# Streaming modulation weights in row pieces behind the input, on one Trainium2 core

## The chip, the cores and the metric

The kernel runs on one core of one Trainium2 chip. The metric is the device time of one execution in microseconds (us); 944.57 us is the median of three runs of the kernel before (942.94 to 949.04).

## The reference

One layer of a hybrid block on x (1024 tokens by 1024 channels), all in float32. Only the first lines matter for this change:

```
mod = c @ w_ada[l] + b_ada[l]                       # 1024 -> 3 x 1024
shift, scale, gate = jnp.split(mod, 3, axis=-1)
h = _rmsnorm(x, norm_g[l]) * (1.0 + scale[:, None, :]) + shift[:, None, :]
proj = h @ w_in[l]                                  # 1024 x 6152 columns
...
x = x + gate[:, None, :] * (merged @ w_out[l])
```

Behind the projection come two attentions with eight heads each (stick-breaking and forgetting), gates, an output projection and a last norm.

## The kernel before

The kernel keeps h transposed in SBUF, channels on partitions, as eight blocks of 128 channels by 1024 tokens. Each block is held as a rounded part and a remainder (`hhi`, `hlo`), and so is each weight (`split`: a copy on ScalarE that rounds, a subtraction that leaves the rest). A product of 128 channels is three matmuls of 128x512 (`mm3`).

The change is in the start, the code under `tc.tile_pool(name="start")`. It is written as small steps, and the string `SEQ` (L44) gives the order in which they are issued; each engine works through its own queue in an order that the scheduler makes from it. A letter is a step, a digit its block:

- `X` loads 128 tokens of x (512 KB). `s` sums their squares on ScalarE. `n` makes the reciprocal root for four of these blocks (`n0` for tokens 0 to 511, `n1` for 512 to 1023): a Ln and an Exp on ScalarE and small steps on VectorE.
- `x` scales a block and turns it on TensorE, 128x128 at a time, eight squares in two PSUM banks; a copy on ScalarE or VectorE (string `CPY`, L41) takes each bank to `xnT`. Blocks in `DIAG` (L38) are not scaled first but multiplied by a diagonal matrix that holds the factors (L268).
- `L` loads modulation weights, `a` multiplies them by c and adds over the eight row blocks on VectorE (`weigh`, L279 and L281), `f` (`factors`) adds over the 128 partitions with a matmul against ones (L292) and makes shift and scale of one channel block on VectorE (L294, L295).
- `m` modulates a block on ScalarE (L301) and splits it. `R` and `w` load and split the first four column blocks of `w_in`; `POOLW` (L39) names those whose subtraction runs on GpSimd.
- `p` multiplies one channel block by the four weights into seven PSUM banks: 21 matmuls of 128x512 for each of the eight blocks, 168 in all.

Before, `L` brings all 1024 rows of 128 columns of shift and of scale (one `L` brings 256), in two DMAs of 512-byte rows, and the loads are mixed with those of x: the first comes ahead of all but one x block. `a`, `f`, `m` and `p` of a channel block follow as its weights are there.

All loads go through SyncE's queue. Its DMAs carry one of eight semaphores, so that a DMA waits for the one eight places ahead of it. The raw weights of `w_in` share three buffers.

Behind the start come 24 matmuls for one more bank (L1011), the values' projection (L530 to L532) and the attentions. There the order of the instructions on every engine is not touched by the change.

Of the kernel before, what the change touches and what calls it, by code (L numbers as in the profile page):

```python
# [8 lines left out]
F32 = mybir.dt.float32  # L9
# [5 lines left out]
ALU = mybir.AluOpType  # L15
# [24 lines left out]
BATCH = (4,)  # L40
CPY = "dd aa aa aa ad dd ad aa"  # L41
GROUPS = ((0,), (1,), (2,), (3, 4), (5,), (6,), (7,))
ADATAG = ("ada1", "ada1b", "ada1", "ada2", "xb1", "ada1b", "ada1")
SEQ = "X2 L0 X0 s0 X1 X3 X4 s3 a0 X7 s2 X6 X5 s1 n0 x0 L1 s4 s5 s7 s6 R0 L2 x2 f0 R2 L3 n1 x1 a3 a1 x3 x4 R1 w0 x5 f1 x7 x6 R3 m0l w1l L6 w1r m0r m1l m1r a2 w3l L5 w2 f2 a5 f3 m2 m3l a6 p0l p1l f4 p0r w3r p1r m3r f5 p2l L7 f6 m4 m5l p2r p3l p3r a7 f7 m6 m5r m7l p4 p5 p6l p6r m7r p7"  # L44
WPOOL = ()
MLAG = 2
GAHEAD = 1
# [21 lines left out]
def tile_hybrid_block(ctx, tc, x, c, w_ada, b_ada, norm_g, w_in, b_forget,  # L69
                      w_o_sb, w_o_fox, b_gate, w_out, final_g, out):  # L70
    nc = tc.nc
    x2 = x[0]
    out2 = out[0]
    wada = w_ada[0]
# [58 lines left out]
    cT = cols[:, 0:8]  # L133
# [25 lines left out]
    def load_raw(src, shape, name="wraw"):  # L159
        raw = wpool.tile(shape, F32, name=name, tag="wraw", bufs=3)  # L160
        nc.sync.dma_start(raw, src)
        return raw

    def split(hi, lo, raw, pool=False):
        nc.scalar.copy(hi, raw)  # L165
        (nc.gpsimd if pool else nc.vector).tensor_sub(lo, raw, hi)  # L166
        return hi, lo

    def load_w(src, shape, pool=False):
# [27 lines left out]
    with tc.tile_pool(name="start", bufs=1) as sp:  # L197
# [2 lines left out]
        xt = [xa[:, t, :] for t in range(4)] + [xb[t // 2][:, t % 2, :] for t in range(4)]  # L200
        xnT = sp.tile([P, KB, S], F32, name="xnT")
        half = {"": slice(0, S), "l": slice(0, 512), "r": slice(512, S)}
        group = {k: g for g in GROUPS for k in g}
        edges = (0,) + BATCH + (TB,)
        batch = {t: b for b in range(len(edges) - 1) for t in range(edges[b], edges[b + 1])}
        adas, ams, raws, norms, sums, wsplit, bank = {}, {}, {}, {}, {}, {}, [0]
# [2 lines left out]
        def load_x(t):  # L209
            nc.sync.dma_start(xt[t], x2[t * P:(t + 1) * P, :])  # L210

        def load_ada(k):
            n = len(group[k]) * P
            tag = ADATAG[GROUPS.index(group[k])]
            ada = sp.tile([P, KB, 2, n], F32, name="ada", tag=tag, bufs=1)
            for j in range(2):
                nc.sync.dma_start(ada[:, :, j, :],
                                  wada[:, j * D + k * P: j * D + k * P + n].rearrange("(q p) n -> p q n", p=P))
            adas[k] = ada

        def load_w0(i):
            raws[i] = load_raw(wcol((QA, KA, GCOL + 8 * P, ZA)[i]), WSH)
# [33 lines left out]
        def turn_x(t):  # L256
            if t in DIAG:
                diag = sp.tile([P, P], F32, name="diag", tag="diag", bufs=2)
                nc.vector.tensor_scalar(diag, ident, norms[t], None, ALU.mult)
            else:  # L260
                (nc.gpsimd if t in POOLX else nc.vector).tensor_scalar(xt[t], xt[t], norms[t], None, ALU.mult)
            for b in range(2):
                copy = nc.scalar.copy if CPY.split()[t][b] == "a" else nc.vector.tensor_copy
                pt = turn_tile(t)
                for k in range(4):
                    o, i = pt[:, k * P:(k + 1) * P], xt[t][:, (4 * b + k) * P:(4 * b + k + 1) * P]
                    if t in DIAG:
# [5 lines left out]
        def weigh(k):

            n = len(group[k]) * P
            if k in PEK:
                return
            o = ams[k] = sp.tile([P, 2, n], F32, name="am", tag="am%d" % n, bufs=2)
            nc.vector.tensor_scalar(o, adas[k][:, 0], cT[:, 0:1], None, ALU.mult)  # L279
            for q in range(1, KB):  # L280
                nc.vector.scalar_tensor_tensor(o, adas[k][:, q], cT[:, q:q + 1], o, ALU.mult, ALU.add)  # L281

        def factors(k):
            k0 = group[k][0]
            pm = acc_tile(2)
            for j in range(2):
                if k in PEK:
                    for q in range(KB):
                        nc.tensor.matmul(pm[:, j:j + 1], adas[k][:, q, j, :], cT[:, q:q + 1], start=q == 0,
                                         stop=q == KB - 1)  # L290
                    continue
                nc.tensor.matmul(pm[:, j:j + 1], ams[k0][:, j, (k - k0) * P:(k - k0 + 1) * P], ones,  # L292
                                 start=True, stop=True)
# [10 lines left out]
        def split_w(i, part):  # L304
# [158 lines left out]
    def largest(p):  # L463


        pt = tp_tile()
        nc.tensor.transpose(pt[0:1, :P], vmost[p], ident)
        top = at.tile([1, 1], F32, name="vtop", tag="vtop", bufs=2)
        nc.vector.tensor_reduce(top, pt[0:1, :P], mybir.AxisListType.X, ALU.max)
        nc.vector.tensor_scalar(top, top, 1e-25, None, ALU.max)  # L470
        e = top.bitcast(I32)
        nc.vector.tensor_scalar(e, e, 0x7F800000, None, ALU.bitwise_and)
        pair = vscale[p] = at.tile([1, 2], F32, name="vpow", tag="vpow", bufs=2)
        nc.vector.tensor_scalar(pair[:, 0:1].bitcast(I32), e, -1.0, float((254 + VSCALE) << 23), ALU.mult, ALU.add)
        nc.vector.tensor_scalar(pair[:, 1:2].bitcast(I32), e, 1.0, float((VSCALE + 15) << 23), ALU.mult, ALU.subtract)

    def spread(p):

        pt = tp_tile()
        nc.tensor.matmul(pt[:, 0:2], ones_row, vscale[p], start=True, stop=True)  # L480
        o = at.tile([P, 2], F32, name="vsc", tag="vsc", bufs=2)
        nc.vector.tensor_copy(o, pt[:, 0:2])
        for q in (p, p + 1):
            vscale[q], vback[q] = o[:, 0:1], o[:, 1:2]

    def sprinkle(units, marks):
# [12 lines left out]
        return units  # L499
# [51 lines left out]
    def load_v(p):  # L551
        vraw[p] = load_raw(vd[p], [P, S], "vraw").rearrange("p (a b d) -> p a b d", a=TB, b=2)
# [471 lines left out]
    for p in range(7):  # L1024
        a, b = [], []
        if p == 0:
            g = sprinkle(gs.pop(0), [(6, lambda: load_v(0)), (8, lambda: largest(0)), (10, lambda: spread(0)),
                                     (13, lambda: take_v(0))])
# [12 lines left out]
        q = p + 1  # L1041
# [39 lines left out]
    for t in range(TB):  # L1081
# [12 lines left out]
        for i, (c0, c1) in enumerate(zip(cuts, cuts[1:])):  # L1094
            n = slice(c0, c1)
# [53 lines left out]
```

## Time and profile before

| | |
|---|---|
| median of three runs | 944.57 us |
| the profiled execution's own time | 944.57 us |
| its span (first to last instruction) | 942.9 us |
| first of the 168 matmuls of the start | 30.96 us |
| first matmul behind them (L1011) | 79.04 us |

Times in rows are microseconds from the start of the span unless a row says ns. PE is TensorE, PEld its weight load, DVE VectorE, ACT ScalarE, POOL GpSimd, SP SyncE. The end of a matmul is modelled: a matmul of 128x512 is shown with some 0.4 us, while the next one starts 0.23 us later. So spacing is read from starts. A float32 matmul (not the rounded kind) shows as two instructions.

### The profile page before, as it was taken

Reading aid. Unit: us, or ns where it says so; the run is one execution under the profiler, and the core shown is the slowest. Engines: PE = TensorE matmul, PEld = TensorE weight load, DVE = VectorE, ACT = ScalarE, POOL = GpSimd, SP = SyncE. Lnnn points to the kernel's source line nnn. Section 1 sums busy time; section 2 is a strip of 40 time slices with the busy share of each in tenths; the row PEclk is TensorE's granted clock in tenths of the full one; section 3 lists DMA queues with packets and bytes.
Section 4 is the critical chain, followed back from the end, with each engine's and each line's share of the span. In section 5 each row is a group of like instructions: output and inputs, shape, how many; then the busy total and the mean of one; then the engine's idle time right before and its main releaser. Section 6 shows DMA issues by size and latency. Waiting matters only on the chain. (4 is left out here: it accounts for less than half of the span.)

```text
span 942.9 us, 14905 instructions
## 1 busy us (share of the span) xinstructions
PE 891.2 (95%) x5282; PEld 753.0 (80%) x5282; DVE 704.8 (75%) x1402; ACT 598.3 (63%) x1102; POOL 115.8 (12%) x191
## 2 busy tenths in 40 slices
PE   2799999999999989999999999999999999999997
PEld 2688978889788868889878787897887777788886
DVE  4984998688786788878798768657687767776544
ACT  5656787776777697897678765445667456553222
POOL 0401001000010000100000112211212212540000
PEclk9999999999999989999999999999999999999999
DMA  9933495544594564936548697967999999552221
GB/s 313 305 98 101 100 225 122 127 104 121 132 193 121 143 152 112 176 82 133 147 121 187 175 211 157 210 160 188 192 203 173 279 263 213 201 178 90 101 92 54
DMA packets 260659, 152.14 MB, mean 161 GB/s; under 512 B 157156, under 2 KB 241748, under 8 KB 260584
## 3 DMA queue, kind: packets, MB, share of 16 engines
q1 hardware_dynamic: 257592, 142.78, 60.5%
q0 software_dynamic: 2880, 8.39, 4.9%
q8 instruction: 41, 0.67, 0.3%
q14 instruction: 34, 0.28, 0.1%
q10 hardware_dynamic: 112, 0.02, 0.0%
HBM read 80.31 MB, written 24.71 MB: 111 GB/s over the span
## 5 line engine op out<-in xcount | busy, mean ns | idle before, releaser
L181 PE MATMUL acc<-hhi,w 128*128 128x512 f32 x584 | 237.4, 406 | 0.0
L183 PE MATMUL acc<-hhi,w 128*128 128x512 f32 x584 | 230.0, 394 | 0.0
L182 PE MATMUL acc<-hlo,w 128*128 128x512 f32 x584 | 229.7, 393 | 0.0
L183 PEld LDWEIGHTS acc<-hhi,w 128*128 128x128 f32 x584 | 110.8, 190 | 24.6
L726 DVE SCALAR_TENSOR_TENSOR pc<-pw,pc 128x1024 f16<-128x1024 f32 (+7 forms) x128 | 96.6, 758 | 43.2 <-ACT pc L722 42.4
L181 PEld LDWEIGHTS acc<-hhi,w 128*128 128x128 f32 x584 | 111.4, 191 | 21.7 <-issue 2.0
L182 PEld LDWEIGHTS acc<-hlo,w 128*128 128x128 f32 x584 | 111.3, 191 | 19.6
L722 ACT ACTIVATE pc<-pw 128x1024 f16<-128x1024 f32 (+7 forms) x128 | 86.8, 679 | 19.2 <-DMA wT<-pc 17.8
L718 ACT ACTIVATE pw<-pw,low 128x1024 f32<-128x1024 f32 (+3 forms) x64 | 49.6, 776 | 73.3 <-DVE low L713 73.3
L766 POOL TENSOR_TENSOR ysb<-ysb,fac 128x128 f32<-128x128 f32 x64 | 35.6, 556 | 452.1 <-DVE ysb L765 388.1
L720 ACT ACTIVATE pw<-pw,low 128x1024 f32<-128x1024 f32 (+3 forms) x64 | 49.5, 774 | 62.1 <-DVE low L713 61.7
L530 PE MATMUL acc<-wv,hhi 128*128 128x256 f32 (+1 forms) x256 | 73.6, 288 | 0.0
L532 PE MATMUL acc<-wv,hlo 128*128 128x256 f32 (+1 forms) x256 | 72.4, 283 | 0.0
L531 PE MATMUL acc<-wv,hhi 128*128 128x256 f32 (+1 forms) x256 | 72.4, 283 | 0.0
L701 DVE SCALAR_TENSOR_TENSOR pw<-z,pw 128x512 f32<-128x512 f32 (+4 forms) x96 | 52.9, 553 | 23.1 <-ACT pw L692 22.6
L756 PE MATMUL pv<-vv,wT 128*128 128x128 f16 x534 | 66.6, 220 | 3.7 <-DVE ysb L765 3.7
L623 PE MATMUL z<-ks,qs 128*128 128x512 f32 (+1 forms) x192 | 66.4, 346 | 2.7 <-DVE yT L778 2.7
L625 PE MATMUL z<-kx,qs 128*128 128x512 f32 (+1 forms) x192 | 65.7, 344 | 3.4 <-DMA kx<-ks 3.4
L757 PE MATMUL pv<-vv,wT 128*128 128x128 f16 x534 | 66.5, 220 | 0.0
L166 DVE TENSOR_TENSOR w<-wraw,w 128x1024 fp32r<-128x1024 f32 x44 | 54.0, 1227 | 10.0 <-ACT w L165 8.8
L757 PEld LDWEIGHTS <-wT 128*128 128x128 f16 x576 | 56.6, 98 | 4.4 <-issue 4.1
L708 DVE TENSOR_TENSOR_SCAN pw<-pw 128x512 f32<-128x512 f32 (+2 forms) x64 | 58.9, 921 | 1.2
(276 smaller groups left out, 1985.8 us busy)
## 6 DMA issues: line engine op xcount, KB each, us to landing
wraw<-in_w_in_dram SPq DMA_DIRECT2D x48, 512.0 KB, 4.7
gd<-stg SPq DMA_DIRECT2D x32, 256.0 KB, 2.6
kx<-ks POOLq DMA_DIRECT2D x28, 256.0 KB, 6.4
ada<-in_w_ada_dram SPq DMA_DIRECT2D x12, 512.0 KB, 7.6
zd<-stg SPq DMA_DIRECT2D x16, 256.0 KB, 2.8
zt<-zd SPq DMA_DIRECT2D x32, 128.0 KB, 2.7
vraw<-vd SPq DMA_DIRECT2D x8, 512.0 KB, 3.9
fb<-fd SPq DMA_DIRECT2D x8, 512.0 KB, 4.6
```

Source lines behind the costliest of these rows:

```text
L181: nc.tensor.matmul(ps, w[0], x[0], start=first, stop=False)
L182: nc.tensor.matmul(ps, w[0], x[1], start=False, stop=False)
L183: nc.tensor.matmul(ps, w[1], x[0], start=False, stop=last)
L530: nc.tensor.matmul(ps[:, a], hhi[k][:, t], hi[:, k, :], start=k == 0, stop=False)
L531: nc.tensor.matmul(ps[:, a], hhi[k][:, t], lo[:, k, :], start=False, stop=False)
L532: nc.tensor.matmul(ps[:, a], hlo[k][:, t], hi[:, k, :], start=False, stop=k == KB - 1)
L623: nc.tensor.matmul(o, qs[p, j][:, tq], ks[p, j][:, s], start=True, stop=False)
L625: nc.tensor.matmul(o, qs[p, j][:, tq], kx[p, j][:, s], start=False, stop=not mask)
L722: nc.scalar.activation(pair.parts(a)[0], w, AF.Copy, scale=WSCALE)
L726: nc.vector.scalar_tensor_tensor(lo, pair.logits(a), WSCALE, hi, ALU.mult, ALU.subtract)
L756: nc.tensor.matmul(y[:, a, :], w[:, b + s, :], v, start=s == 0, stop=False)
L757: nc.tensor.matmul(y[:, a, :], w[:, b + nb + s, :], v, start=False, stop=s == nb - 1)
```

## The change

`L` now brings pieces of 256 rows by 512 columns of shift and of scale, in two DMAs of 2048-byte rows: eight pieces, the first four for channel blocks 0 to 3, the last four for blocks 4 to 7, in three buffers. All x blocks are loaded ahead of them. `a` makes two VectorE steps of 128x1024 for a piece. The factors of blocks 0 to 3 are made together when their four pieces are weighed, and so are those of blocks 4 to 7. x blocks 5 and 7 are also turned with a diagonal; all bank copies but the two of block 0 run on ScalarE; all subtractions of the weights run on VectorE. A new step `d` (`warm`) issues four float32 matmuls of 128x512 into a bank that nothing reads; `d0` and `d1` stand behind the turns and ahead of the factors. The preload of the values' weights is put behind the last split.

```diff
-DIAG = (1, 4, 6)
-POOLW = (0, 1, 2, 3)
+DIAG = (1, 4, 5, 6, 7)
+POOLW = ()
-CPY = "dd aa aa aa ad dd ad aa"
-GROUPS = ((0,), (1,), (2,), (3, 4), (5,), (6,), (7,))
-SEQ = "X2 L0 X0 s0 X1 X3 X4 s3 a0 X7 s2 X6 X5 s1 n0 x0 L1 s4 ...
+CPY = "dd aa aa aa aa aa aa aa"
+SEQ = "X2 X0 s0 X1 X3 X4 s3 X7 s2 X6 X5 s1 L0 L1 n0 x0 L2 s4 s5 s7 s6 a0 x2 L3 R0 n1 x1 a1 x3 x4 R1 a2 L4 w0 x5 x7 x6 d0 d1 a3 R2 L5 f0 m0l w1l f1 ...
-        def load_ada(k):
...
+        def load_ada(i):
+
+            ada = adas[i] = sp.tile([P, 2, 2, 512], F32, name="ada", tag="ada", bufs=3)
+            rows_ = wada[i % 4 * 2 * P:(i % 4 + 1) * 2 * P, :]
             for j in range(2):
+                c0 = j * D + i // 4 * 512
+                nc.sync.dma_start(ada[:, :, j, :], rows_[:, c0:c0 + 512].rearrange("(q p) n -> p q n", p=P))
...
+        def weigh(i):
+
+            g = i // 4
+            if i % 4 == 0:
+                ams[g] = sp.tile([P, 2, 512], F32, name="am", tag="am", bufs=2)
+            for x in range(2):
+                q = i % 4 * 2 + x
+                if q == 0:
+                    nc.vector.tensor_scalar(ams[g], adas[i][:, x], cT[:, 0:1], None, ALU.mult)
+                else:
+                    nc.vector.scalar_tensor_tensor(ams[g], adas[i][:, x], cT[:, q:q + 1], ams[g], ALU.mult, ALU.add)
...
+        def warm(k):
+
+            o = acc_tile(2)
+            for i in range(4):
+                nc.tensor.matmul(o, ident, xnT[:, k, 512:1024], start=i == 0, stop=i == 3)
...
-    first_v[0].preload()
+    with tc.issue_after(last_split[0].ins), tc.issue_after(last_split[1].ins):
+        first_v[0].preload()
```

`warm` and `factors` both take the one PSUM bank of `acc_tile(2)`.

On TensorE, at the end of the turns (L270 and L268 before, L266 after), the kernel before has:

```order
L270 MATMUL z<-ident,xb_169 128x128 x4
L270 MATMUL tp<-ident,xb_170 128x128 x4
L181 MATMUL z<-hhi,wqk 128x512
L270 MATMUL acc<-ident,xb_170 128x128 x4
L181 MATMUL acc<-hhi,wz 128x512
L268 MATMUL z<-diag,xb_170 128x128 x4
L268 MATMUL tp<-diag,xb_170 128x128 x4
```

and the changed one:

```order
L266 MATMUL z<-diag,xb_170 128x128 x4
L266 MATMUL tp<-diag,xb_170 128x128 x4
L324 MATMUL acc<-xnT,ident 128x512 x8
L286 MATMUL acc<-ones,am 128x1 x8
L180 MATMUL z<-hhi,wqk 128x512 x2
L180 MATMUL acc<-hhi,wz 128x512
```

The first projections (L181, now L180) stood between the last turns; now they stand behind the eight unread matmuls (L324) and behind the factors' matmuls of four channel blocks (L286).

On VectorE, around the factors of the blocks that TensorE needs first, the kernel before has (`am_399` and `am_284` are weighed sums, `hlo_157` and `hlo_158` the remainders of blocks 0 and 1):

```order
L166 TENSOR_TENSOR hlo_157<-xnT_171,hhi_149 128x512
L166 TENSOR_TENSOR hlo_158<-xnT_171,hhi_150 128x512
L279 TENSOR_SCALAR am_284<-ada_259,cols_128 128x512
L281 SCALAR_TENSOR_TENSOR am_399<-ada_236,cols_128,am_399 128x256
L281 SCALAR_TENSOR_TENSOR am_284<-ada_259,cols_128,am_284 128x512
...
L294 TENSOR_TENSOR ashf_142<-acc_417,cols_128 128x1
L295 SCALAR_TENSOR_TENSOR amul_141<-acc_417,b_scale1_132,cols_128 128x1
```

and the changed one (`am_228` is the sum of pieces 0 to 3, `am_401` that of pieces 4 to 7, `wz_407` the third weight):

```order
L281 SCALAR_TENSOR_TENSOR am_228<-ada_244,cols_128,am_228 128x1024 x2
L165 TENSOR_TENSOR wqk_312<-wraw_247,wqk_312 128x1024
L165 TENSOR_TENSOR wqk_312<-wraw_305,wqk_312 128x256
L165 TENSOR_TENSOR wqk_312<-wraw_305,wqk_312 128x768
L279 TENSOR_SCALAR am_401<-ada_309,cols_128 128x1024
L281 SCALAR_TENSOR_TENSOR am_401<-ada_309,cols_128,am_401 128x1024
L288 TENSOR_TENSOR ashf_142<-acc_368,cols_128 128x1
L289 SCALAR_TENSOR_TENSOR amul_141<-acc_368,b_scale1_132,cols_128 128x1
L288 TENSOR_TENSOR ashf_142<-acc_378,cols_128 128x1
L289 SCALAR_TENSOR_TENSOR amul_141<-acc_378,b_scale1_132,cols_128 128x1
L165 TENSOR_TENSOR wz_407<-wraw_363,wz_407 128x1024
L288 TENSOR_TENSOR ashf_142<-acc_394,cols_128 128x1
```

The subtractions of the weights (L165) came from GpSimd, and the third one now stands between the factors of block 1 and those of block 2.

On SyncE's queue, the kernel before begins with:

```order
L210 DMA xa_168<-in_x_dram 128x1024
L217 DMA ada_173<-in_w_ada_dram 128x8x128 x2
L210 DMA xa_168<-in_x_dram 128x1024 x3
L210 DMA xb0_169<-in_x_dram 128x1024
L210 DMA xb1_170<-in_x_dram 128x1024 x2
```

and the changed one with (`wraw` are the first weights of `w_in`):

```order
L209 DMA xa_168<-in_x_dram 128x1024 x4
L209 DMA xb0_169<-in_x_dram 128x1024
L209 DMA xb1_170<-in_x_dram 128x1024 x2
L209 DMA xb0_169<-in_x_dram 128x1024
L217 DMA ada_189<-in_w_ada_dram 128x2x512 x2
L217 DMA ada_192<-in_w_ada_dram 128x2x512 x2
L217 DMA ada_216<-in_w_ada_dram 128x2x512 x2
L217 DMA ada_244<-in_w_ada_dram 128x2x512 x2
L159 DMA wraw_247<-in_w_in_dram 128x8x128
```

Two transfers of modulation weights that stood behind the first x block now stand behind the last one.

## Rows read from the trace of the kernel before

**Rows 1.** The page: busy time by engine, then slices of the span (40)
```profile
PE 891.2 (95%) x5282; PEld 753.0 (80%) x5282; DVE 704.8 (75%) x1402; ACT 598.3 (63%) x1102; POOL 115.8 (12%) x191
...
PE   2799999999999989999999999999999999999997
...
DMA  9933495544594564936548697967999999552221
```

**Rows 2.** Busy time of stretches: from:to, length, engines, PEclk, DMA share, GB/s
```profile
0.00:9.00 9.00, 0.31 (x1) 0.18 (x1) 0.64 (x5) 1.28 (x1) 1.09 (x8) 1.00 0.84 251
9.00:18.00 9.00, 1.01 (x4) 0.92 (x4) 5.12 (x18) 6.74 (x13) 0.00 (x0) 1.00 1.05 389
36.50:42.90 6.40, 3.67 (x17) 2.71 (x17) 6.37 (x9) 1.55 (x3) 3.98 (x3) 1.00 1.18 289
42.90:46.30 3.40, 3.40 (x9) 2.63 (x9) 3.29 (x6) 2.91 (x3) 1.11 (x1) 0.50 1.14 289
60.00:79.05 19.05, 19.05 (x88) 15.84 (x87) 9.82 (x20) 6.68 (x10) 0.00 (x0) 1.00 0.14 30
```

**Rows 3.** Timeline, 9 to 30 us: start, length, engine, line, operation [idle <-releaser]
```profile
9.46 1.06 ACT L242 ACTIVATE sq<-xa 128x1024 bf16<-128x1024 f32 x1 [7.37 <-DMA xa<-in_x_dram]
...
12.10 1.06 ACT L242 ACTIVATE sq<-xa 128x1024 bf16<-128x1024 f32 x1 [1.50 <-DMA xa<-in_x_dram]
...
17.70 1.41 DVE L261 TENSOR_SCALAR xa<-xa,inv 128x1024 f32<-128x1024 f32 x2
...
18.51 1.12 PE L270 MATMUL tp<-ident,xa 128*128 128x128 f32 x4 [4.31 <-DVE xa L261]
...
23.76 0.21 ACT L251 ACTIVATE inv<-inv 128x4 f32<-128x4 f32 x1
...
26.13 1.14 PE L268 MATMUL z<-diag,xb 128*128 128x128 f32 x8
...
27.10 1.06 PE L268 MATMUL tp<-diag,xb 128*128 128x128 f32 x8
```

**Rows 4.** Timeline, 30 to 80 us
```profile
30.96 0.48 PE L181 MATMUL z<-hhi,wqk 128*128 128x512 f32 x1
...
39.59 0.39 PE L182 MATMUL z<-hlo,wqk 128*128 128x512 f32 x1
42.18 0.61 PE L292 MATMUL acc<-ones,am 128*128 128x1 f32 x4 [2.21 <-DVE am L281]
...
42.83 0.16 DVE L294 TENSOR_TENSOR ashf<-acc,cols 128x1 f32<-128x1 f32 x1
42.90 0.21 DVE L295 SCALAR_TENSOR_TENSOR amul<-acc,b_scale,cols 128x1 f32<-128x1 f32 x1
...
48.67 0.39 PE L181 MATMUL acc<-hhi,wz 128*128 128x512 f32 x1
48.90 0.50 PE L292 MATMUL acc<-ones,am 128*128 128x1 f32 x4
49.26 0.48 PE L181 MATMUL pv<-hhi,w 128*128 128x512 f32 x1
...
79.04 0.39 PE L181 MATMUL acc<-hhi,w 128*128 128x512 f32 x1
```

**Rows 5.** Groups by line and shape: count | busy us, mean ns | idle before
```profile
L166 DVE TENSOR_TENSOR wv<-wraw,wv 128x1024 fp32r<-128x1024 f32 x8 | 9.6, 1221 | 0.0
L599 DVE SCALAR_TENSOR_TENSOR gacc<-wraw,cols,gacc 128x1024 f32<-128x1024 f32 x7 | 9.0, 1282 | 10.7 <-DMA wraw<-in_w_ada_dram 10.7
L597 DVE TENSOR_SCALAR gacc<-wraw,cols 128x1024 f32<-128x1024 f32 x1 | 0.7, 743 | 0.0
L166 DVE TENSOR_TENSOR hlo<-xnT,hhi 128x512 fp32r<-128x512 f32 x10 | 7.5, 766 | 2.1 <-ACT hhi L165 2.1
...
L271 ACT COPY xnT<-z 128x512 f32<-128x512 f32 x4 | 2.3, 586 | 0.8 <-PE z L270 0.6 <-PE z L268 0.2
```

**Rows 6.** Timeline of TensorE around a float32 matmul of 128x512
```profile
647.59 1.02 PE L606 MATMUL tp<-gacc,ones 128*1 128x512 f32 x2
648.54 0.50 PE L181 MATMUL acc<-hhi,w 128*128 128x512 f32 x1
```

**Rows 7.** Busy time of stretches around a later fall of the clock
```profile
343.30:346.70 3.40, 1.03 (x5) 0.38 (x3) 3.37 (x8) 3.34 (x8) 0.00 (x0) 1.00 0.49 103
346.70:353.50 6.80, 6.32 (x16) 5.04 (x17) 4.45 (x14) 5.45 (x14) 0.65 (x1) 0.50 0.59 149
```

More of the change, by code (lines that the diff above doesn't have):

```diff
@@ L30 @@
 FP = 2
-PEK = ()
 EVACS = "k0 z0 g0 g1 q0 k1 q1"
@@ L37 @@
 POOLX = ()
-DIAG = (1, 4, 6)
-POOLW = (0, 1, 2, 3)
+DIAG = (1, 4, 5, 6, 7)
+POOLW = ()
 BATCH = (4,)
-CPY = "dd aa aa aa ad dd ad aa"
-GROUPS = ((0,), (1,), (2,), (3, 4), (5,), (6,), (7,))
-ADATAG = ("ada1", "ada1b", "ada1", "ada2", "xb1", "ada1b", "ada1")
-SEQ = "X2 L0 X0 s0 X1 X3 X4 s3 a0 X7 s2 X6 X5 s1 n0 x0 L1 s4 s5 s7 s6 R0 L2 x2 f0 R2 L3 n1 x1 a3 a1 x3 x4 R1 w0 x5 f1 x7 x6 R3 m0l w1l L6 w1r m0r m1l m1r a2 w3l L5 w2 f2 a5 f3 m2 m3l a6 p0l p1l f4 p0r w3r p1r m3r f5 p2l L7 f6 m4 m5l p2r p3l p3r a7 f7 m6 m5r m7l p4 p5 p6l p6r m7r p7"
+CPY = "dd aa aa aa aa aa aa aa"
+SEQ = "X2 X0 s0 X1 X3 X4 s3 X7 s2 X6 X5 s1 L0 L1 n0 x0 L2 s4 s5 s7 s6 a0 x2 L3 R0 n1 x1 a1 x3 x4 R1 a2 L4 w0 x5 x7 x6 d0 d1 a3 R2 L5 f0 m0l w1l f1 w1r m0r m1l m1r f2 R3 a4 L6 w2 f3 m2 m3l w3l p0l p1l a5 L7 p0r w3r p1r m3r p2l a6 a7 f4 f5 p2r p3l p3r f6 f7 m4 m5l m6 m5r m7l p4 p5 p6l p6r m7r p7"
 WPOOL = ()
@@ L162, in load_raw @@
         return raw
+    last_split = []
     def split(hi, lo, raw, pool=False):
-        nc.scalar.copy(hi, raw)
-        (nc.gpsimd if pool else nc.vector).tensor_sub(lo, raw, hi)
+        last_split[:] = [nc.scalar.copy(hi, raw), (nc.gpsimd if pool else nc.vector).tensor_sub(lo, raw, hi)]
         return hi, lo
@@ L202, in tile_hybrid_block @@
         half = {"": slice(0, S), "l": slice(0, 512), "r": slice(512, S)}
-        group = {k: g for g in GROUPS for k in g}
         edges = (0,) + BATCH + (TB,)
@@ L210, in load_x @@
             nc.sync.dma_start(xt[t], x2[t * P:(t + 1) * P, :])
-        def load_ada(k):
-            n = len(group[k]) * P
-            tag = ADATAG[GROUPS.index(group[k])]
-            ada = sp.tile([P, KB, 2, n], F32, name="ada", tag=tag, bufs=1)
+        def load_ada(i):
+            ada = adas[i] = sp.tile([P, 2, 2, 512], F32, name="ada", tag="ada", bufs=3)
+            rows_ = wada[i % 4 * 2 * P:(i % 4 + 1) * 2 * P, :]
             for j in range(2):
-                nc.sync.dma_start(ada[:, :, j, :],
-                                  wada[:, j * D + k * P: j * D + k * P + n].rearrange("(q p) n -> p q n", p=P))
-            adas[k] = ada
+                c0 = j * D + i // 4 * 512
+                nc.sync.dma_start(ada[:, :, j, :], rows_[:, c0:c0 + 512].rearrange("(q p) n -> p q n", p=P))
         def load_w0(i):
@@ L271, in turn_x @@
                 copy(xnT[:, 4 * b:4 * b + 4, t * P:(t + 1) * P], pt.rearrange("p (a b) -> p a b", a=4))
[L273 to L281, printed above, removed]
+        def weigh(i):
[8 more added lines that the diff above has]
+                    nc.vector.scalar_tensor_tensor(ams[g], adas[i][:, x], cT[:, q:q + 1], ams[g], ALU.mult, ALU.add)
         def factors(k):
-            k0 = group[k][0]
             pm = acc_tile(2)
             for j in range(2):
[L287 to L292, printed above, removed]
+                nc.tensor.matmul(pm[:, j:j + 1], ams[k // 4][:, j, k % 4 * P:(k % 4 + 1) * P], ones,
                                  start=True, stop=True)
@@ L324, in project @@
                         proj_mm(accs[i][hf], wsplit[i], hf, k, k == 0, k == KB - 1)
-        todo = dict(X=load_x, L=load_ada, R=load_w0, s=square, n=norm, x=turn_x, a=weigh, f=factors, m=modulate,
+        def warm(k):
+            o = acc_tile(2)
+            for i in range(4):
+                nc.tensor.matmul(o, ident, xnT[:, k, 512:1024], start=i == 0, stop=i == 3)
+        todo = dict(d=warm, X=load_x, L=load_ada, R=load_w0, s=square, n=norm, x=turn_x, a=weigh, f=factors, m=modulate,
                     w=split_w, p=project)
```

## The prediction

> **What bounds the kernel now.** I read the page first. TensorE is busy for 95% of the span, and only the first slice of 40 shows a 2 and the second a 7 [rows 1]: the kernel is bound by TensorE, and what it loses, it loses in the start. Behind the start the order on every engine is the same in both kernels, so the question is one number: when do the 168 matmuls of the start end? Before, the next matmul starts at 79.04, and the first of the 168 at 30.96 [rows 4].
>
> The stretch from 60.00 to 79.05 is dense: TensorE is busy for all of its 19.05 us with 88 instructions, of which four are those of one factors step [rows 2]; 84 matmuls in 19.05 us are 0.227 us each. So 168 need 38.1 us, and before they are spread over 48.1: 10.0 us are lost. The timeline shows where: the second half of x is still being turned between them, TensorE stands still from about 40.0 to 42.18 for a weighed sum on VectorE [rows 4], and at 42.90 the granted clock falls to 0.50 (1.2 instead of 2.4 GHz) for 3.4 us, in which nine instructions start instead of fifteen [rows 2]: 6 x 0.227 = 1.4 us. In the 6.4 us ahead of that fall TensorE had been busy for 3.67 and VectorE for 6.37. VectorE is what holds the start back.
>
> The changed kernel's question is then: when does its first projection matmul start (I call it T), and how dense are the 168 from there? Break-even is T = 79.04 - 38.1 = 40.9 less whatever is lost behind T.
>
> **The change part by part.**
>
> x first. Before, the square of the x block that is the sixth transfer starts at 12.10, that of the fourth at 9.46 [rows 3]; both wait for DMA. Two transfers of 0.524 MB leave the front. At the 389 GB/s of 9 to 18 us [rows 2] they are worth 2.7 us, at the 251 of 0 to 9 us 4.2. I take 3.1, near the rate of the stretch in which that block lands. VectorE's first scaling then moves from 17.70 to 14.6 and the first turn from 18.51 to 15.4. ScalarE's Exp of the second norm, at 23.76 + 0.21 before [rows 3], ends at 20.9; three small steps (0.2 each) and a diagonal (0.3) later, at 21.8, TensorE can turn block 4. Blocks 0 to 3 are through by then.
>
> Turns of blocks 4 to 7. All four are now multiplied by a diagonal: eight banks, spaced 0.97 us as at 26.13 and 27.10 [rows 3], say 1.0: 8.1 us, to 29.9. The diagonals of blocks 7 and 6 stand on VectorE behind weighing steps of 1.28 us each, but two of those fit into the 4 us that two blocks take on TensorE. ScalarE's copies of a bank take 0.59 [rows 5], less than the 1.0 between banks.
>
> Weighing. Pieces 0 to 3 are one step of 0.74 (L597's row) and seven of 1.28 (L599's row, the same operation and shape) [rows 5]: 9.7 us of VectorE, from about 18 to 30.6 with the norm's steps and the diagonals between. The pieces land in time: x ends near 13.5, four pieces of 1.05 MB take 11.0 us at an estimated 380 GB/s. The trace of before has no rows of 2048 bytes; the nearest are 289 GB/s for the 512-byte rows of 36.5 to 42.9 and 389 for the stretch of 9 to 18, most of it 4096-byte rows of x [rows 2]. On SyncE's queue piece 3 waits until VectorE has weighed piece 0 (about 20) and frees its buffer; the first weights of `w_in` stand behind it. Piece 2 is then still in flight, so I cost that at nothing; uncovered it would be a microsecond or two. At 289 GB/s the fourth piece lands some 3.5 us later and the sums are ready at about 31 to 32. Either way T does not move, for the reason that follows.
>
> Eight unread matmuls. They stand ahead of the factors on TensorE. A float32 matmul of 128x512 takes two passes: before, one starts at 647.59 and the next instruction at 648.54, 0.95 us [rows 6]; two passes without the fill at either end are 0.43 each, 0.86. Eight are 6.9 (to 7.6) us: 29.9 to 36.9, rounded. So the weighed sums, ready at 30.6, wait for TensorE. Below nothing this cannot be: nothing of the 168 can start ahead of them. At the lower clock it would be 13.8.
>
> What lies beside them. The four subtractions of weights that come from GpSimd cost VectorE 1.22 each [rows 5]; two of them and the first two steps of piece 4 (0.74 + 1.28) run from about 31.5, when ScalarE is done with copies and has rounded the first weight, to 36. The unread matmuls hide them. Without that cover T could not be below some 38.5, so the unread matmuls themselves delay T by about two us, not by seven.
>
> Factors. All four use one bank, so each pair of matmuls waits until VectorE has read the one ahead. At 42.18 before, VectorE's add starts 0.65 after the matmul and the second step ends 0.28 behind that [rows 4], about 1.0 in all with the handover. Factors 0: 36.9 to 37.9; factors 1: to 38.95. Then VectorE has the third weight's subtraction (1.22) in its queue: 40.15. Factors 2's reads end at 40.5, factors 3's matmuls run to 41.0, and only then come projections in TensorE's queue. ScalarE has the first rounded block by about 40. T = 41.0.
>
> Behind T. The first remainder (0.77 for 512 columns [rows 5]) is ready some 1.3 us after T and four matmuls fill 0.9: 0.4 lost. The second block's remainder stands behind a weighing step: 0.4. The sums of pieces 4 to 7 are ready on VectorE at about 56.2, TensorE comes to them at 55.6: 0.6, 1.4 (rounded) in all. Four factors steps among the projections cost 0.36 each, as at 48.67 to 49.26 (0.59 between two matmuls instead of 0.227) [rows 4]: 1.4.
>
> The sum: 41.0 + 38.1 + 1.4 + 1.4 = 81.9, against 79.04: 2.9 later. Everything behind moves by as much: the profiled execution would take 944.57 + 2.9 = 947.5 us. Its own time is the median of the three runs (944.57), 1.7 over its span, so no correction is due. The moved preload of the values' weights costs nothing: they are needed behind 82 us, and their splits are through by about 72, hidden by the last projections.
>
> **The rivals.**
>
> A, the clock falls at T. The trace shows that a stretch in which TensorE is little busy (1.03 of 3.40 us) is followed by one at 0.50 [rows 7], and the same happened behind the wait at 40 us. In the changed kernel TensorE has only factors matmuls from 36.9 to 41.0. For it: the gap is longer than the 2.2 us that sufficed before. Against it: eight small matmuls lie in it, and the unread ones just ahead. It would cost the 1.4 us worked out above: 948.9. The Trainium skill (TensorE: Matmul & The Clock Gate, "HAM oscillation — how this bites in real kernels") says that a wait of TensorE throttles it to the half rate and that the next burst then starts slow; by that rule this rival is the likelier one, and the eight unread matmuls stand on the wrong side of the wait. The trace agrees as far as its falls all follow a little busy stretch; it does not show whether the factors' matmuls would count.
>
> B, the unread matmuls run at the lower clock. Then they take 13.8 us, T is 6.9 later, 954.4, and with A's fall 955.8. It decides if the turns do not hold the clock up. Against it: before, with less work on TensorE in the turns, the stretch behind them still shows a granted 1.00 (2.4 GHz) from 36.5 to 42.9 [rows 2].
>
> C, not slower. The clock fell in before once more for long, from 346.70 to 353.50, 6.8 us at half speed, 3.4 us lost [rows 7]. The instructions there stay in order, but that fall follows a wait which depends on when transfers land; if it does not come back in the changed kernel, or for half as long, 2.9 later in the start is paid back: 947.5 - 3.4 = 944.1. It decides from 2.9 us on, that is if nearly the whole fall goes. For it: three runs of before differ by 6 us, so something of this size comes and goes. Against it: nothing in the change touches that place.
>
> That the change does not do what it says, a scheduler that puts projections ahead of the unread matmuls, is excluded by the order shown above.
>
> **How the numbers follow.** My forecast 0.42, A 0.33, B 0.08, C 0.17. The likeliest is 947.5. Its own range: x earlier by 4.2 instead of 3.1 (-1.1) and no waits behind T (-1.4) give 945.0; 0.95 for an unread matmul (+0.7), x by 2.7 only (+0.4) and waits twice as long (+1.4) give 950.0. C pulls the low end to 943.0 (944.1 with the first of the two gains), A with the upper ends and the runs' spread the high end to 953.0; most of B stays outside. A measurement of this kernel tells about 1% (9.4 us) from no change. Faster by more than that: no case reaches 935.1, 0.02. Slower by more: B, 0.07. Within 1%: 0.91.
>
> **What would show it.** Right: the first turn near 15.4; eight unread matmuls (16 instructions) spaced 0.43 us that end near 37 with the sums of pieces 0 to 3 ready before they do; the first projection near 41; a factors chain of about 4 us with one 1.2 us subtraction in it; the first L1011 matmul near 82; GpSimd idle through the start. A shows as a granted clock of 0.50 behind 40 us, B as unread matmuls spaced 0.86, C as a stretch near 350 us at 1.00. I am wrong in the mechanism if VectorE's sums, not the unread matmuls, end last ahead of the factors, if the weights' DMAs do, or if the time behind the start differs by more than the shift.

## The result and the profile after

The changed kernel takes 949.49 us (median of 19 executions, 947.61 to 956.02). The kernel before, run beside it, takes 944.44 (19 executions, 940.66 to 950.38). The ratio is 1.0054 with a 95% interval of 1.0035 to 1.0073: slower by 5 us, 3.3 to 6.9, half a per cent: clear of zero, and inside the 1% in which the forecast put it. The forecast of 947.5 us is 2.0 below the median; rival A's 948.9 is nearer. The profiled execution is the median one (949.49; span 947.8).

The page of the changed kernel, where [rows 1] is that of before:

```profile
PE 902.1 (95%) x5314; PEld 758.9 (80%) x5314; DVE 695.6 (73%) x1364; ACT 599.4 (63%) x1106; POOL 105.0 (11%) x185
...
PE   3999999999999989999999899899999998999996
...
PEclk9899999999999989999999899999999999999999
DMA  9904485834585464834559696968988999552321
```

TensorE has 32 instructions more: the 16 of the unread matmuls, and 16 because two more x blocks are turned with a diagonal (eight instructions a bank instead of four). Its first two slices show 3 and 9 instead of 2 and 7, and yet the end is later: a busy TensorE is not a TensorE at work on the 168. The second slice now has an 8 in the granted clock.

Busy time of stretches of the changed kernel (from:to, length, engines, PEclk, DMA share, GB/s), to be read beside [rows 2] and [rows 7]:

```profile
18.00:30.00 12.00, 12.00 (x95) 11.08 (x94) 10.75 (x16) 9.24 (x19) 0.00 (x0) 1.00 1.07 346
30.00:36.05 6.05, 5.94 (x14) 2.13 (x12) 4.46 (x5) 2.41 (x4) 0.00 (x0) 1.00 1.08 349
36.05:39.27 3.22, 1.82 (x12) 1.56 (x12) 1.87 (x7) 2.19 (x4) 0.00 (x0) 1.00 1.10 348
39.27:46.09 6.82, 6.74 (x18) 5.49 (x19) 5.68 (x10) 6.82 (x11) 0.00 (x0) 0.50 1.08 338
46.10:60.00 13.90, 13.90 (x67) 11.47 (x66) 8.57 (x13) 4.13 (x6) 0.00 (x0) 1.00 0.16 45
60.00:83.07 23.07, 23.07 (x108) 19.24 (x106) 7.96 (x12) 9.20 (x14) 0.00 (x0) 1.00 0.11 24
...
349.90:356.70 6.80, 5.78 (x15) 4.62 (x16) 4.45 (x12) 5.42 (x16) 0.65 (x1) 0.50 0.57 146
```

The factors' chain runs from 36.06 to 40.22. In its first 3.22 us TensorE is busy for 1.82, and the granted clock is 0.50 (1.2 instead of 2.4 GHz) from 39.27 on for 6.8 us: one us ahead of the first projection. Behind that, from 46.10 to 83.07, TensorE is busy without a hole. Rival A's fall is there and is twice as long as the one in the start of before. Rival C's fall is there too (349.90 instead of 346.70). GpSimd is idle in all the stretches of the start shown.

The timeline of the changed kernel (start, length, engine, line, operation), beside [rows 3] and [rows 4]:

```profile
14.88 1.12 PE L268 MATMUL tp<-ident,xa 128*128 128x128 f32 x4 [7.20 <-DVE xa L259]
...
25.49 3.92 DVE L281 SCALAR_TENSOR_TENSOR am<-ada,cols,am 128x1024 f32<-128x1024 f32 x3
...
27.70 1.06 PE L266 MATMUL tp<-diag,xb 128*128 128x128 f32 x8
...
28.60 7.40 PE L324 MATMUL acc<-xnT,ident 128*128 128x512 f32 x16
...
30.36 2.43 DVE L165 TENSOR_TENSOR wqk<-wraw,wqk 128x1024 fp32r<-128x1024 f32 x3 [0.95 <-ACT wqk L165]
...
36.06 0.61 PE L286 MATMUL acc<-ones,am 128*128 128x1 f32 x4
...
37.04 0.61 PE L286 MATMUL acc<-ones,am 128*128 128x1 f32 x4 [0.37 <-DVE amul L289]
37.08 1.52 ACT L295 ACTIVATE xnT<-xnT,ashf,amul 128x512 f32<-128x512 f32 x2 [1.07 <-DVE amul L289]
...
37.88 1.22 DVE L165 TENSOR_TENSOR wz<-wraw,wz 128x1024 fp32r<-128x1024 f32 x1
38.02 0.61 PE L286 MATMUL acc<-ones,am 128*128 128x1 f32 x4 [0.38 <-DVE amul L289]
...
39.35 1.01 PE L286 MATMUL acc<-ones,am 128*128 128x1 f32 x4 [0.72 <-DVE amul L289]
...
40.22 1.20 PE L180 MATMUL z<-hhi,wqk 128*128 128x512 f32 x2
...
83.07 0.39 PE L180 MATMUL acc<-hhi,w 128*128 128x512 f32 x1
```

The weighed sums are complete at 29.41 (25.49 + 3.92), and the unread matmuls run from 28.60 to 36.0. The four factors steps start at 36.06, 37.04, 38.02 and 39.35, the first projection (T) at 40.22, and the next matmul behind the 168 at 83.07: 4.03 later than the 79.04 of before [rows 4]. From T it takes 42.85 us instead of the 40.9 that the sum gave.

### The profile page after: what moved, and what is told of

Read it like the earlier page. It is cut to its first block, busy times and chain, and to the rows that moved or that the text cites. A ratio compares the mean times of both kernels' runs of the same rounds, so it can differ in the third digit from the quotient of the medians.

```text
span 947.8 us, 14934 instructions
## 1 busy us (share of the span) xinstructions
PE 902.1 (95%) x5314; PEld 758.9 (80%) x5314; DVE 695.6 (73%) x1364; ACT 599.4 (63%) x1106; POOL 105.0 (11%) x185
## 5 line engine op out<-in xcount | busy, mean ns | idle before, releaser
L180 PE MATMUL acc<-hhi,w 128*128 128x512 f32 x584 | 237.6, 407 | 0.0
L181 PE MATMUL acc<-hlo,w 128*128 128x512 f32 x584 | 229.9, 394 | 0.0
L180 PEld LDWEIGHTS acc<-hhi,w 128*128 128x128 f32 x584 | 111.7, 191 | 21.7 <-issue 2.0
L181 PEld LDWEIGHTS acc<-hlo,w 128*128 128x128 f32 x584 | 111.4, 191 | 19.7
L165 DVE TENSOR_TENSOR w<-wraw,w 128x1024 fp32r<-128x1024 f32 (+2 forms) x46 | 55.3, 1203 | 8.7 <-ACT w L165 7.4
```

Source lines behind the costliest of these rows:

```text
L180: nc.tensor.matmul(ps, w[0], x[0], start=first, stop=False)
L181: nc.tensor.matmul(ps, w[0], x[1], start=False, stop=False)
```

## The experiments

The unread matmuls are no part of the reference, so leaving them out leaves out nothing. Three numbers are read from each profile: T, the end of the start (the first matmul behind the 168), and the time between. e7's end is the 169th matmul by count: its scheduler put four of the 24 matmuls that follow the start into it, at 57.10 to 57.78. The times of e6, e8 and e9 are single executions; each ratio is to the kernel before run beside it (medians 944.4 to 946.1).

| kernel | T | end of the start | between | clock at 0.50 in the start, from (us long) | span | median, us | ratio to before (95%) |
|---|---|---|---|---|---|---|---|
| before | 30.96 | 79.04 | 48.1 | 42.9 (3.4) | 942.9 | 944.44 | |
| before, again (e8) | 31.84 | 81.66 | 49.8 | 52.2 (3.4) | 942.4 | 944.06 | |
| changed | 40.22 | 83.07 | 42.85 | 39.3 (6.8) | 947.8 | 949.49 | 1.0054 (1.0035 to 1.0073) |
| changed, again (e9) | 40.67 | 82.44 | 41.8 | 41.3 (3.4) | 948.2 | 949.96 | |
| e1 | 35.83 | 78.85 | 43.0 | 33.4 (6.8) | 944.7 | 948.73 | 1.0035 (1.0017 to 1.0054) |
| e2 | 41.54 | 83.11 | 41.6 | 41.5 (3.4) | 952.5 | 953.83 | 1.0079 (1.0057 to 1.0101) |
| e3 | 34.19 | 76.39 | 42.2 | 32.1 (6.8) | 942.5 | 946.02 | 0.9990 (0.9972 to 1.0009) |
| e4 | 37.12 | 77.43 | 40.3 | 33.0 (3.4) | 946.6 | 948.29 | 1.0017 (0.9995 to 1.0040) |
| e5 | 29.34 | 82.31 | 53.0 | 47.2 (6.8) | 946.9 | 949.66 | 1.0047 (1.0027 to 1.0066) |
| e6 | 47.83 | 89.33 | 41.5 | 47.2 (3.4) | 951.3 | 953.03 | |
| e7 | 35.90 | 76.14 | 40.2 | none | 945.3 | 946.63 | 1.0015 (1.0000 to 1.0030) |
| e10 | 39.95 | 83.05 | 43.1 | 39.3 (6.8) | 952.2 | 955.07 | 1.0105 (1.0079 to 1.0131) |

### e1: no unread matmuls

```diff
-... x5 x7 x6 d0 d1 a3 R2 ...
+... x5 x7 x6 a3 R2 ...
```

> The changed kernel without the eight unread matmuls. My prediction said they delay the first projection T by about two us only, because VectorE's queue holds the factors until 36 anyway: T then goes from 40.15 to about 38.5 and the start ends (first L1011 matmul) at about 81.5. Rival: VectorE takes the factors up earlier once their matmuls come earlier (the scheduler puts them between the weights' subtractions), and the unread matmuls delay T by nearly all of their 7.4 us: T about 34.5, start's end about 77 to 78.5, total about 944 to 945. In both, TensorE waits longer without work, so a fall of the granted clock to 0.50 of at least as long (6.8 us) is expected.

The start ends 4.2 us earlier than in the changed kernel. Timeline of e1:

```profile
30.22 0.60 PE L286 MATMUL acc<-ones,am 128*128 128x1 f32 x4 [0.70 <-DVE am L281]
...
31.11 1.23 DVE L165 TENSOR_TENSOR wqk<-wraw,wqk 128x1024 fp32r<-128x1024 f32 x1 [0.95 <-ACT wqk L165]
32.26 0.15 DVE L288 TENSOR_TENSOR ashf<-acc,cols 128x1 f32<-128x1 f32 x1
...
33.43 0.95 DVE L165 TENSOR_TENSOR wqk<-wraw,wqk 128x768 fp32r<-128x768 f32 x1
...
35.83 1.63 PE L180 MATMUL z<-hhi,wqk 128*128 128x512 f32 x3
```

With the unread matmuls gone, the first factors matmuls start at 30.22, as soon as the sums are there, and the scheduler puts the factors' steps on VectorE between the three subtractions instead of behind them and behind piece 4. So the subtractions do not hold T at 38.5. The chain starts 5.8 us earlier than in the changed kernel, and takes 5.6 us instead of 4.2, since a subtraction now stands in it and the clock falls: 4.4 us are left for T. The fall comes at 33.4, when TensorE has had only factors to do since the turns, and the time from T to the end is 43.0. The ratio goes from 1.0054 to 1.0035 only, some 1.8 us, and the two intervals overlap.

### e2 and e3: the factors of four blocks in one step

```diff
+        def factors(g):
             pm = acc_tile(2)
-            for j in range(2):
-                nc.tensor.matmul(pm[:, j:j + 1], ams[k // 4][:, j, k % 4 * P:(k % 4 + 1) * P], ones,
-                                 start=True, stop=True)
+            for k in range(4):
+                for j in range(2):
+                    nc.tensor.matmul(pm[:, 4 * j + k:4 * j + k + 1], ams[g][:, j, k * P:(k + 1) * P], ones,
+                                     start=True, stop=True)
```

VectorE then makes all four blocks' factors in three steps of 128x4; f0 and f1 stand for f0 to f3 and f4 to f7. e2 keeps the unread matmuls, e3 drops them.

> The changed kernel with the factors of four channel blocks made by one pair of steps (one bank, eight matmuls in a row, three small VectorE steps of 128x4), so that no factors matmul waits for VectorE. If the chain of four factors holds T (as predicted, 36.06 to 40.15), T comes 1 to 3 us earlier. Rival: ScalarE's first modulation and rounding (about 2.3 us behind the first factors) would have ended at 39.2 anyway, so T gains only 0.5 to 1: T 39.2 to 39.6. Clock: the wait of TensorE stays about 3 us, so the fall at T may stay; start's end 80 to 82.5.

> Both: no unread matmuls and one factors step for four blocks. If the unread matmuls are what ends last, T is about 34 and the start ends at about 76 to 78; if VectorE's queue holds, T is about 37.5 to 38. The clock falls in both theories, as TensorE has nothing from 29 to T.

Timeline of e2:

```profile
36.95 1.95 PE L287 MATMUL acc<-ones,am 128*128 128x1 f32 x16
...
39.46 1.52 ACT L297 ACTIVATE xnT<-xnT,ashf,amul 128x512 f32<-128x512 f32 x2 [3.46 <-DVE amul L292]
40.88 1.12 ACT L165 CAST hhi<-xnT 128x512 fp32r<-128x512 f32 x2
...
41.54 1.22 PE L180 MATMUL z<-hhi,wqk 128*128 128x512 f32 x2 [2.64 <-ACT hhi L165]
```

The four handovers between TensorE and VectorE go, and nothing is won: T is 41.54, later than either expectation. Of the 1.3 us, 0.9 are there before the factors (36.95 instead of 36.06; the unread matmuls start at 29.49 instead of 28.60). All eight matmuls (16 instructions) now stand ahead of block 0's factors, so ScalarE starts to modulate at 39.46 instead of 37.08, and its modulation and rounding, 2.1 us, end last ahead of T: 4.6 us from the factors to T, instead of 4.2. In the changed kernel the chain of steps 1 to 3 runs beside ScalarE's work on block 0.

Timeline of e3:

```profile
29.35 1.95 PE L287 MATMUL acc<-ones,am 128*128 128x1 f32 x16 [0.71 <-DVE am L281]
...
34.19 1.22 PE L180 MATMUL z<-hhi,wqk 128*128 128x512 f32 x2 [2.89 <-ACT hhi L165]
```

In e3 the same step starts at 29.35, straight behind the sums, T is 34.19, and the start ends at 76.39, 2.7 to 5.3 us earlier than in the two profiles of before. By time it is no different from before (0.9990), and its interval lies apart from that of the changed kernel: the eight unread matmuls and the four separate factors steps are together worth the changed kernel's half per cent, though the factors in one step (e2) win nothing alone, and leaving out the unread matmuls (e1) isn't told apart from the changed kernel.

### e4 and e7: unread matmuls in the wait instead of ahead of it

```diff
-... x5 x7 x6 a3 R2 L5 f0 m0l ...
+... x5 x7 x6 a3 R2 L5 f0 d0 m0l ...
```

e4 is e3 with four unread matmuls behind the factors, in the factors' bank. e7 is e3 with one step of one and one of three unread matmuls, written into the bank of the fourth weight, which is not in use yet; the scheduler put two ahead of the factors and two behind:

```diff
-... x5 x7 x6 a3 R2 L5 f0 m0l ...
+... x5 x7 x6 d1 a3 R2 L5 f0 d3 m0l ...
```

> As the one before, but with four unread float32 matmuls (3.7 us) behind the factors' matmuls instead of eight ahead of them: they lie in TensorE's wait. If the clock at T is set by that wait, the fall of the granted clock goes or shrinks, and the start ends 1.5 to 3 us ahead of the kernel without unread matmuls, T being the same within 0.5 us. Rival: the clock falls all the same (or costs nothing), and the start ends no earlier than there.

> One factors step for four blocks, and four unread matmuls in a bank of their own: one ahead of the factors, where TensorE waits 0.7 us for the weighed sum anyway, and three behind them, in the 2.9 us wait for the first rounded block. T stays at 34.2 to 34.8 if they run at full clock. If TensorE's want of work between 28.7 and 34.2 is what lowers the clock, the fall is gone or half as long, and the start ends at 74.5 to 75.5 (76.39 without them), total 1 to 4 us below before. Rival: factors' matmuls of one column do not count as work, the clock falls all the same, the three run at half speed as in the kernel with four behind, T is 36 to 37 and the start ends at 76 to 78.

Timeline of e4 from the factors to the first projection:

```profile
29.91 1.95 PE L287 MATMUL acc<-ones,am 128*128 128x1 f32 x16 [0.70 <-DVE am L281]
...
32.32 5.37 PE L326 MATMUL acc<-xnT,ident 128*128 128x512 f32 x8 [0.46 <-DVE amul L291]
...
37.12 0.79 PE L180 MATMUL z<-hhi,wqk 128*128 128x512 f32 x1
```

The same stretch of e7:

```profile
29.39 1.98 PE L325 MATMUL pv<-xnT,ident 128*128 128x512 f32 x4 [0.68 <-ACT xnT L269]
...
31.21 1.84 PE L287 MATMUL acc<-ones,am 128*128 128x1 f32 x16
32.91 1.96 PE L325 MATMUL pv<-xnT,ident 128*128 128x512 f32 x4
...
35.90 1.02 PE L180 MATMUL z<-hhi,wqk 128*128 128x512 f32 x3 [1.02 <-ACT hhi L165]
```

In e4 the clock falls at 33.0 all the same, 0.7 us into the unread matmuls: eight instructions take 5.37 us instead of 3.4, and T is 2.9 later than in e3. The fall is over before T, so from T to the end it is 40.3 us. In e7 TensorE waits for 0.68 and 1.02 us instead of e3's 0.71 and 2.89, the clock stays at 1.00 until 346 us, and from T to the end it is 40.2. That is one profile; but over e7's 12 executions the mean granted clock is 0.9893, against 0.9863 over e3's 10, 5.7 us less at 0.50. e7 pays 1.7 us in T for the 2.0 that it saves: nothing is left.

What a fall costs is read from the starts of the 168, as the time by which those in it exceed 0.227 us each: 2.8 us in the changed kernel and 3.0 in e10, where nearly all of a fall of 6.8 lies behind T; 2.1 and 2.3 in e1 and e3, where 4.4 and 4.7 us of it do; 1.4 to 1.7 for the falls of 3.4 (e2, e6, e9). Outside the falls the 168 lose 1.7 to 2.2 us in all these kernels, e4 and e7 among them, but for e1 (2.7).

### e6: sixteen unread matmuls

```diff
-... d0 d1 a3 ...
+... d0 d1 d2 d3 a3 ...
```

> The changed kernel with sixteen unread matmuls instead of eight. If they stand on the path, T moves by the full price of eight more, 7.4 us (40.2 to 47.5), since VectorE's queue is empty by then; less the clock, if the longer work changes where it falls. Rival: part of it is still hidden, T moves by 5 us or less.

Timeline of e6:

```profile
29.14 14.92 PE L324 MATMUL acc<-xnT,ident 128*128 128x512 f32 x32
44.12 0.61 PE L286 MATMUL acc<-ones,am 128*128 128x1 f32 x4
...
47.83 1.20 PE L180 MATMUL z<-hhi,wqk 128*128 128x512 f32 x2
```

Eight more take 7.5 us (14.92 - 7.40), T is 7.6 later and the end of the start 6.3, as this fall has half the length: the full price. And with twice as many ahead of the factors the clock still falls, at 47.2, in the last factors step. With none (e1), eight and sixteen unread matmuls ahead of the factors' chain it falls in each of the four profiles.

### e5 and e10: GpSimd's part alone

```diff
-POOLW = (0, 1, 2, 3)
+POOLW = ()
```

e5 is the kernel before with this edit alone; e10 is the changed kernel with the line of before back.

> The kernel before with one part of the change alone: the four weights' subtractions run on VectorE. VectorE gains the time in which GpSimd slowed it (the diagonal of 2.39 us instead of 0.28, and 128x512 steps of 1.02 instead of some 0.7) and pays four subtractions of 1.22. If VectorE's queue is what holds the start of before, the two nearly cancel: start's end 78 to 81 (79.04 before), total within 0.3% of before. Rival: GpSimd's work was what made the start late, and without it the start ends at 76 or earlier.

> The changed kernel with the weights' subtractions back on GpSimd, nothing else edited. Theory 1 (the unread matmuls end last ahead of the factors, and the factors' chain on VectorE sets what follows): the matmuls still run 28.6 to 36.0; the one subtraction of 1.22 us leaves the chain, first projection 39.0 to 39.3 instead of 40.2, end of the start 1 to 2 us earlier, 81.5 to 82.1 with the fall of the clock. Theory 2 (GpSimd's subtractions of 2.8 to 3.1 us stretch what VectorE does beside them, and the first remainder of a weight comes late): a weighing step or a remainder of 0.8 to 1.3 us shows as 2 to 3.5 us beside GpSimd, first projection 40 or later, holes behind it, end of the start 83 or later. In both the rest behind the start stays within 855 to 864 us.

e5 is slower than before by 1.0047, and its start ends at 82.31, beyond both of its views; as that of before ended at 81.66 in a second profile, what the edit does to the start itself isn't shown. e10 is slower too, 1.0105. Timeline of e10:

```profile
30.58 5.25 POOL L165 TENSOR_TENSOR wqk<-wraw,wqk 128x1024 fp32r<-128x1024 f32 x3 [28.85 <-ACT wqk L165]
...
34.20 2.72 DVE L281 SCALAR_TENSOR_TENSOR am<-ada,cols,am 128x1024 f32<-128x1024 f32 x1
...
36.23 0.61 PE L286 MATMUL acc<-ones,am 128*128 128x1 f32 x4
...
39.17 0.91 PE L286 MATMUL acc<-ones,am 128*128 128x1 f32 x4 [0.38 <-DVE amul L289]
...
39.95 1.20 PE L180 MATMUL z<-hhi,wqk 128*128 128x512 f32 x2
```

Both views of e10's expectation were half right; T and the end of the start are about where the second put them. The subtraction leaves the factors' chain, whose last step starts 2.94 us after the first instead of 3.29: it had cost 0.35, not 1.22, because VectorE stood idle for most of that time anyhow, waiting for TensorE's next pair. A weighing step beside GpSimd takes 2.72 us where it takes 1.28 alone, but it is done before the factors come. The Trainium skill (SBUF — State Buffer, "🔬 SBUF: two separate sides") says that a VectorE operation with two SBUF inputs and a GpSimd operation that reads SBUF lock each other out of a shared port, each for its whole instruction; the row nearly agrees, as 34.20 to the end of GpSimd's work at 35.83 and 1.28 more make 2.9. Start and T are the same as in the changed kernel (83.05, 39.95 against 83.07, 40.22); the 4.4 us more of the profiled span lie behind the start, in an order that is the same.

### e8 and e9: both kernels again

Nothing is edited.

> The kernel before once more, for a second profile of it. The start should end within 0.3 us of 79.04, since its order is fixed; what lies behind the start (858.4 us in the first profile, 859.3 in the changed kernel, 860 to 864 in the others) shows how much of the total is not the start's. If it comes out at 858 to 859 again, the changed starts cost something later; if it spreads over several us, it is chance.

> The changed kernel a second time, nothing edited. The kernel before showed its 169th matmul at 79.04 in one profile and 81.66 in another, and its remainders beside GpSimd's subtractions were stretched differently. Theory (the spread of the start comes from collisions with GpSimd and from where the clock falls): without GpSimd the start repeats; first projection 40.2 within 0.5, the clock falls at 39 to 40 for 6.8 us, end of the start 83.1 within 0.7. Rival (the start spreads whatever runs in it, by the landing of the transfers): first projection or end of the start off by 1.5 us or more.

The start of before ends at 79.04 in one profile and at 81.66 in the other (within 0.3 was expected), that of the changed kernel at 83.07 and 82.44. Timeline of e8:

```profile
37.47 3.10 POOL L166 TENSOR_TENSOR wqk<-wraw,wqk 128x256 fp32r<-128x256 f32 x2 [3.71 <-ACT wqk L165]
37.66 3.47 DVE L166 TENSOR_TENSOR hlo<-xnT,hhi 128x512 fp32r<-128x512 f32 x2
```

In e8 two remainders take 3.47 us on VectorE beside 3.10 on GpSimd, where they take 1.28 in the first profile. But there GpSimd's work meets the four weighing steps behind them, 4.25 us instead of e8's 2.19, so that VectorE loses about as much in both. The collision falls on other steps from one profile to the next; what makes the 2.6 us between the two starts isn't shown. That of the changed kernel repeats within 0.7 us. In e9 the fall in the start has half its length, and the one near 350 us does not come; one comes at 478 us instead. Busy time of stretches of e9:

```profile
39.27:46.09 6.82, 6.10 (x23) 4.79 (x24) 6.08 (x12) 6.82 (x12) 0.00 (x0) 0.75 1.07 334
...
349.90:356.70 6.80, 6.76 (x31) 5.44 (x32) 4.44 (x14) 5.48 (x14) 0.65 (x1) 1.00 0.83 141
...
478.20:485.00 6.80, 5.41 (x14) 4.45 (x15) 6.67 (x15) 5.66 (x7) 0.40 (x1) 0.50 0.23 68
```

### The time behind the start

From the end of the start to the end of the span, with the time that the clock stood at 0.50 in it up to 930 us, all kernels having one order there but for the four matmuls of e7 (the expectations of e8 and e10 count to an earlier end, 5.4 us before the span's in the first two profiles):

| time at 0.50, us | behind the start, us (kernel) |
|---|---|
| 10.2 | 860.7 (e8), 862.0 (e6) |
| 13.7 | 863.8 (before), 864.5 (e5), 865.8 (e1) |
| 17.1 | 864.7 (changed), 865.8 (e9), 866.1 (e3), 869.1 (e7), 869.4 (e2) |
| 20.5 | 869.1 (e4), 869.2 (e10) |

The rest is no constant: it spreads over 8.7 us, and it grows with the time at 0.50. From the first row to the last the clock stands low for 10.3 us longer, which at half speed is at most 5.1 us lost, and the mean grows by 7.8; what makes the other 2.7 isn't settled. Where it arises can be read from the traces, start by start: for 170 us behind the start (to about 250 us) TensorE keeps the same pace in all profiles within 0.3 us, but for e4 and e7, which lose 1.1 and 1.7, and from 820 to 930 us within 0.1; the last 12 us differ by up to 0.9. The rest of the differences comes between 250 and 820 us, for the most part in steps at the places where one profile has a fall and another has none. Such a step can exceed what the clock takes (2.7 us at e5's fall of 3.4 us near 481, against e8, which has none there), so the waits around it differ too. So e3 and e7, whose starts end 2.7 to 5.5 us earlier than those of before, are no faster: the rest behind them is 2 to 8 us longer than behind before's.

## Why the prediction was right

**T and the order of things: right.** First turn 14.88 (forecast 15.4), last bank 28.6 (29.9), sums 29.41 ahead of the unread matmuls' end at 36.0 (30.6 and 36.9), T 40.22 (41.0). x came 3.6 us earlier instead of 3.1 (first square of the sixth transfer at 8.48 instead of 12.10 [rows 3]).

**Eight unread matmuls: the length right, their net cost wrong.** 7.40 us against 6.9: the 16 instructions are spaced 0.43 as forecast, and of the other half microsecond 0.3 goes where the second four wait for the bank of the first four. But the step "the unread matmuls themselves delay T by about two us, not by seven" failed: e1 shows 4.4 for T and 4.2 for the end, and further ones cost their full length (e6). The prediction took VectorE's queue as it stood with the unread matmuls in it for the cover; without them the scheduler makes another queue.

**The factors' chain: the sum right, its terms not.** 4.16 us against 4.1. Three steps of 0.98 are as forecast; the third weight's subtraction costs 0.35 more instead of 1.2 (e10); and the last step's four instructions take 0.87 to T, since the clock falls just ahead of it (0.47 in e9, where it falls later).

**From T to the end: the term of the waits failed, rival A came.** Forecast 38.1 + 1.4 + 1.4 = 40.9 without a fall; the changed kernel needs 42.85 and 41.8, by a fall that starts at 39.3 or 41.3. In the first profile 14 of the 168 start between T and 46.23, where they take 6.0 us instead of 3.2: 2.8 lost in the fall. The other 154 take 36.8 us instead of 35.0, with TensorE busy throughout: 1.9 lost, all at four factors steps like this one, against the 1.4 of the forecast.

```profile
56.68 0.50 PE L286 MATMUL acc<-ones,am 128*128 128x1 f32 x4
```

The 1.4 of waits for remainders and sums do not show. So the end came within 1.2 us of the sum in part by luck: T 0.8 early, no waits (1.4) and dearer factors steps (0.5) stand against a fall of 2.8 that the forecast did not have. Rival A, at 0.33, was what happened; its price of 1.4 fits the shorter fall (1.5), the longer one costs twice that. What spoke against it in the forecast, the unread matmuls just ahead, counted for nothing: they end at 36.0, and the clock falls behind 1.82 busy us of 3.22. The rule that the prediction cited there, from the Trainium skill (TensorE: Matmul & The Clock Gate, "HAM oscillation — how this bites in real kernels"), agrees with the changed kernel's two profiles: behind the wait for the factors the projections start slow, in e9 from 0.6 us behind T on. In e7, where unread matmuls shorten the wait, no fall came.

**The start: about right.** By the first profiles +4.0 against +2.9 forecast, by the mean of two each (82.75 less 80.35) +2.4. No run sets the parts of the new start (x first, row pieces, more diagonals, copies on ScalarE) against each other, so what the row pieces are worth by themselves isn't shown.

**"Everything behind moves by as much": wrong as a step.** In the first pair of profiles 0.9 us more are lost behind the start, in the second 5.1. By the prediction's own sign (the time behind the start differs by more than the shift) the first pair bears the step out, 0.9 against 4.0, and the second does not, 5.1 against 0.8. The medians differ by 5.1 us, so some 2.7 by the mean start are not the start's. Part is the clock: its mean over the 19 executions of the changed kernel is 0.9874, or 24 us at 0.50 (twice 1.26% of the span), against 0.9888, or 21 us, over the 25 of before that were run beside e1. That is 3 us more at half speed, 1.5 us lost, of which the start's own falls are a share, and so is the very end of the span, where TensorE has nothing left to do and the clock is low in every profile. The remainder stays open: in the first 170 us behind the start the changed kernel's two profiles lose 0.1 and 0.2 us against e8, and beyond that no run tells the shift from the spread that one kernel shows by itself.

**Rival B is out** (spacing 0.43, clock at 1.00 up to 39.3), **and so is C**: the fall near 350 us came back with its full 6.8 us in the first profile, and where it did not, others took its place.

**GpSimd: not forecast as a cost of its own.** Its removal alone makes the kernel before slower (e5), and putting it back does not help the changed one (e10).

## What to carry to other kernels

Work that only keeps TensorE busy never paid here: ahead of the wait it costs most of its length or all of it, and the clock falls all the same (e1, e6), behind the factors it met the fall itself (e4), and split around them it kept the clock up and cost in T what that saved (e7). When an operation is said to be covered by another engine's queue, write down that queue again without the operation, since a scheduler will. And before a few microseconds are put down to an edit, profile each kernel twice: here the untouched rest of the program moved by up to 8.7 us.

## What the runs showed that was not expected

From 15 to 21 us, where nothing but 2048-byte rows moves in the changed kernel, the transfers ran at 388 GB/s, as the forecast had estimated (380); from 18 to 39 us it is 346 to 349, because the 512-byte rows of `w_in` are mixed in, which alone run at 288 (26 to 27 us), as in before [rows 2]. Unread matmuls ahead of a wait, eight or sixteen, did not keep the clock up through it; in e4 TensorE shows as busy with the factors from 29.91 to 31.86, and the fall comes at 33.0. And one kernel's granted clock takes different courses from one execution to the next: of the falls of the changed kernel's two profiles between 80 and 930 us, three in one and four in the other, only the one near 595 us is common.
